# Layer 1's feed-forward with four gate and up pairs as seven products, and weight sums formed in layer 0: a one-core Trainium2 trunk

## The chip, the cores and the metric

The program runs on one core of one Trainium2 chip. The metric is device microseconds of the whole execution. The kernel before took 2606.74 us, the median of three runs (2606.5 to 2606.75). The profile is one further execution of it.

## The reference

A two-layer trunk over 256 tokens and 16 meta tokens in front of them, model width 2048, everything in float32:

```
h = concat(meta, x)                                  # 272 x 2048
h = h + ssd_mixer(rmsnorm(h))                        # layer 0: Mamba-2 SSD, inner width 4096
h = h + swiglu(rmsnorm(h), w_gate_up[0], w_down[0])
k, v = rmsnorm(h) @ w_kv                             # shared keys and values
h = h + stick_breaking_attention(rmsnorm(h), w_q, k, v, w_o)   # layer 1
h = h + swiglu(rmsnorm(h), w_gate_up[1], w_down[1])
out = rmsnorm(h)[16:]

swiglu(u, wgu, wd) = (silu((u @ wgu)[:, :5632]) * (u @ wgu)[:, 5632:]) @ wd
```

Layer 1's feed-forward, on 256 tokens, is where most of the change lies.

## The kernel before, in words

**Number format.** A float32 product is three TensorE products: each operand is split into a rounded part `hi` (type fp32r) and a remainder `lo`, and hi x lo, hi x hi and lo x hi are added up in PSUM. ScalarE makes a weight's `hi` (L128), VectorE its `lo` (L129). Tokens are split once per stage and stay in SBUF (`u`, `hid`).

**Weights.** Each weight block of 128 x 1024 (512 KB) comes by one DMA on SyncE's queue (SP) into one of five `raw` buffers (`load`, L111), is split into one of five `hi` and one of four `lo` buffers (`halves`), and serves 24 matmuls (`mac`, L142 to L144: eight pieces of 128 x 128, three each). A projection (`project`, L152) to 128 outputs has two blocks and 48 matmuls, each with the weight piece stationary and all tokens moving (272 columns in layer 0, 256 in layer 1's feed-forward). `project_block` does several projections side by side.

**Layer 0's feed-forward** (`ffn0`, L599) runs 44 gate and 44 up projections and the down projections in two parts of the hidden rows (`PARTS`). Each projection's split, products and collection follow one another in program order; SP, ACT, DVE and PE run ahead of each other as far as the buffers go. After the first block of a projection a caller may have something done (`then`).

**Layer 1's feed-forward** (L817 to the end) has two kinds of work interleaved:

- gate and up projections by `project` for hidden block m = 0 to 43, loop at L1034. Two neighbouring blocks make one hidden pair j = m // 2; `keep` (L874) forms the four token-and-row blocks of the pair, their sums (`sm`), and their `hi` and `lo` in the buffer `sa`.
- the down projection for a pair j of hidden rows and a group g of 512 output columns as a "quad": a product of two 2 x 2 block matrices in seven block products in place of eight (the scheme of Strassen and Winograd). Here the tokens (`sa`) are stationary and the weights, 256 columns, are moving. `quad` (L911) loads the weight's four blocks (`raw`), forms four differences of them on VectorE (`tt`, L918 to L920), splits blocks and differences (`split`, `less`, L892 to L900), and issues 7 x 3 = 21 matmuls (L904) into four PSUM banks `x0` to `x3`. A run of pairs (`RUNS`: 0 to 4, 5 to 10, 11 to 16, 17 to 21) stays in the banks; at its end `gather` (L955) combines the banks and adds to the residual `res`.

Which quad comes when is set by a small planner: `tick` is called twice per projection and `step` issues the next quad if its rows were kept at least `LAG` ticks ago and the running `debt` (an account with the entries of `WORK`) is below `ROOM`. The first ticks transpose the residual (`turn`, L842), since from then on tokens stand on partitions.

**The last run** (L1056 to the end, pairs 17 to 21) is written out by hand: for column group 0 quads, for groups 1 to 3 eight plain products (`plain`, `products`), with the final norm of the finished groups between them; `part` (L1115) does group 3 piece by piece, and `collect` (L968) adds each finished bank to the residual.

**Short matmuls.** `short` (L837) issues two matmuls of 128 columns at the first quad of each run's group 0 and behind each block of transposes in `turn`; `beat` (L147) issues three at chosen places of the projections.

**Element-wise lines named below**: L958 to L962 and L965 are the combination and the residual add in `gather`, L971 is `collect`, L990 the multiplication by the final norm's weight, L1073 the last scaling.

## Time and profile before

| | before |
|---|---|
| median of three runs | 2606.74 us |
| profiled execution | 2606.56 us |
| its span (first to last instruction) | 2604.8 us |
| mean granted TensorE clock | 0.999 |
| bytes moved | 482.5 MB, 185 GB/s on average |

The stages by the trace: state-space mixer to about 730 us, layer 0's feed-forward to about 1501 us, keys, values, attention and output projection to 1896 us, layer 1's feed-forward from there to the end, of which the last run from 2544 us.

How to read it: PE is TensorE's matmul, PEld its weight load, DVE is VectorE, ACT is ScalarE, POOL is GpSimd and SP is SyncE, whose queue (SPq) issues the DMAs. A matmul's row shows the time from its issue to its end; since matmuls overlap, what one costs is the step to the next one's start. A row of the groups of instructions has the line, engine, operation, tiles, the count, the busy time, the mean of one in ns, and the idle time of that engine ahead of them with what ended it.

### The profile page before, as it was taken

To read this page: it belongs to the slowest core of one execution; us is meant where nothing else is said; L and a number is where in the kernel's file an instruction comes from. 1 tells how busy PE (TensorE), PEld (TensorE's weight loads), DVE (VectorE), ACT (ScalarE), POOL (GpSimd) and SP (SyncE) were. 2 spreads that over 40 slices of the span, in tenths; PEclk is the share of its full clock that TensorE was granted. 3 is DMA by queue.
4 is the path that set the end of the run, shared out by engine and by line. 5 is a ranking of instruction groups with operands and counts; after the bars stand their busy time and mean duration, and the time that the engine had idled before them with its cause. 6 is when DMAs were issued, how large, how long until landed. Compare 5 with 4: busy or idle time off the path is not lost.

```text
span 2604.8 us, 52246 instructions
## 1 busy us (share of the span) xinstructions
PE 2595.8 (100%) x21767; PEld 2589.3 (99%) x21767; DVE 1838.8 (71%) x2777; ACT 1373.7 (53%) x1948; POOL 6.2 (0%) x26
## 2 busy tenths in 40 slices
PE   9999999999999999999999999999999999999998
PEld 9999999999999999999999999999999999999998
DVE  8888777768855554445555576666666988989998
ACT  6766657556544443334444454444554555555554
POOL 0000000000000000000000000000000000000000
PEclk9999999999999999999999999999999999999999
DMA  7666656565555555555555555555656656566665
GB/s 256 201 186 187 185 174 188 175 186 182 170 178 179 178 178 179 178 179 178 178 179 166 185 182 159 169 169 157 192 178 195 201 190 211 194 202 202 209 203 170
DMA packets 159597, 482.47 MB, mean 185 GB/s; under 512 B 21824, under 2 KB 43264, under 8 KB 159360
## 3 DMA queue, kind: packets, MB, share of 16 engines
q1 hardware_dynamic: 159072, 478.86, 58.3%
q8 instruction: 170, 2.79, 0.4%
q14 instruction: 67, 0.55, 0.1%
q10 hardware_dynamic: 288, 0.28, 0.0%
HBM read 476.91 MB, written 2.17 MB: 184 GB/s over the span
## 4 chain that ended last, share of the span: by engine, by line
PE 99%; ACT 0%; DVE 0%; DMA 0%; issue 0%; SPq 0%; DVEq 0%
PE pp L144 29%; PE pp L143 29%; PE pp L142 29%; PE x L904 7%; PE pp L904 1%; PE py L536 1%; PE py L542 0%; PE pt L449 0%; PE pb L725 0%; PE pt L319 0%; PE psc L694 0%; PE pe L143 0%; PE pe L142 0%; PE pe L144 0%; PE pc L491 0%; DMA raw<-w_first 0%
## 5 line engine op out<-in xcount | busy, mean ns | idle before, releaser
L128 ACT CAST hi<-raw 128x1024 fp32r<-128x1024 f32 (+1 forms) x802 | 832.6, 1041 | 899.9 <-PE pp L143 733.9
L129 DVE TENSOR_TENSOR lo<-raw,hi 128x1024 fp32r<-128x1024 f32 (+1 forms) x802 | 964.8, 1206 | 274.2 <-issue 121.5
L142 PE MATMUL pp<-u,hi 128*128 128x272 f32 (+1 forms) x4064 | 1147.8, 282 | 0.0
L143 PE MATMUL pp<-u,hi 128*128 128x272 f32 (+1 forms) x4064 | 1145.9, 282 | 0.0
L144 PE MATMUL pp<-u,lo 128*128 128x272 f32 (+1 forms) x4064 | 1145.4, 282 | 0.1
L143 PEld LDWEIGHTS pp<-u,hi 128*128 128x128 f32 x4064 | 763.0, 188 | 0.5 <-issue 0.4
L142 PEld LDWEIGHTS pp<-u,hi 128*128 128x128 f32 x4064 | 763.0, 188 | 0.4
L144 PEld LDWEIGHTS pp<-u,lo 128*128 128x128 f32 x4064 | 762.6, 188 | 0.5 <-DVE lo L129 0.3
L142 PE MATMUL pp<-hid,hi 128*128 128x272 f32 x704 | 201.7, 287 | 0.0
L144 PE MATMUL pp<-hid,lo 128*128 128x272 f32 x704 | 201.7, 287 | 0.0
L143 PE MATMUL pp<-hid,hi 128*128 128x272 f32 x704 | 201.7, 286 | 0.0
L904 PE MATMUL x<-hi,sa 128*128 128x256 f32 x1062 | 184.3, 276 | 0.0
L904 PEld LDWEIGHTS x<-hi,sa 128*128 128x128 f32 x1062 | 159.9, 188 | 0.0
L142 PE MATMUL pp<-ukv,hi 128*128 128x272 f32 x512 | 147.4, 288 | 0.0
L142 PE MATMUL pp<-y,hi 128*128 128x272 f32 x512 | 147.3, 288 | 0.0
L144 PE MATMUL pp<-y,lo 128*128 128x272 f32 x512 | 146.7, 287 | 0.0
L143 PE MATMUL pp<-y,hi 128*128 128x272 f32 x512 | 146.7, 286 | 0.0
L144 PE MATMUL pp<-ukv,lo 128*128 128x272 f32 x512 | 146.1, 285 | 0.0
L143 PE MATMUL pp<-ukv,hi 128*128 128x272 f32 x512 | 146.1, 285 | 0.0
L896 ACT CAST hi<-tt 128x1024 fp32r<-128x1024 f32 x73 | 76.8, 1052 | 123.4 <-PE pp L143 63.1
L144 PEld LDWEIGHTS pp<-hid,lo 128*128 128x128 f32 x704 | 132.6, 188 | 0.0
L142 PEld LDWEIGHTS pp<-hid,hi 128*128 128x128 f32 x704 | 132.6, 188 | 0.0
(302 smaller groups left out, 3612.6 us busy)
## 6 DMA issues: line engine op xcount, KB each, us to landing
raw<-w_gu SPq DMA_DIRECT2D x352, 512.0 KB, 3.6
raw<-w_in SPq DMA_DIRECT2D x152, 512.0 KB, 3.6
raw<-w_dn SPq DMA_DIRECT2D x88, 512.0 KB, 3.9
raw<-w_down SPq DMA_DIRECT2D x80, 512.0 KB, 3.4
raw<-w_out SPq DMA_DIRECT2D x64, 512.0 KB, 3.8
raw<-w_kv SPq DMA_DIRECT2D x64, 512.0 KB, 3.5
raw<-w_q SPq DMA_DIRECT2D x32, 512.0 KB, 3.5
raw<-w_o SPq DMA_DIRECT2D x32, 512.0 KB, 3.6
```

What stands on the lines that cost most here:

```text
L128: S.copy(hi[:, :n, :m], raw[:, :n, :m])
L129: V.tensor_tensor(out=lo[:, :n, :m], in0=raw[:, :n, :m], in1=hi[:, :n, :m].bitcast(F32), op=ALU.subtract)
L142: PE.matmul(ps[:, :n], wh, xl, start=first, stop=False)
L143: PE.matmul(ps[:, :n], wh, xh, start=False, stop=False)
L144: PE.matmul(ps[:, :n], wl, xh, start=False, stop=last)
L536: pin(PE.matmul(py[i * HD:(i + 1) * HD, c0:c1], xd[b][:, 2 * j + i, :], gm[b][:, 2 * j + i, :], start=True, stop=True))
L896: S.copy(hi[:, :n], src[:, :n])
L904: PE.matmul(ps, st[x][:, b], w[y][:, c], start=f, stop=l, skip_group_check=True)
```

## The change

**In layer 0's feed-forward**, 85 "jobs" are worked off. A job loads one block of layer 1's weights into a buffer `sr`, forms the same four differences of it as a quad does (`differences`, result `st`), and stores the 512 KB to DRAM (`sums`). `ahead` is called after the first weight block of each projection, and by `PACE` = 0.8 four calls in five take a job. 32 jobs are for the gate and up weights in a new layout (`w_sg`), 53 for blocks of `w_dn`.

**In layer 1**, the hidden pairs 3, 7, 11 and 15 (`SEVEN`) no longer get their gate and up values by `project`. `run_u` does such a pair as eight units of seven products, through the same function as a quad (`seven`), with the tokens of `u` and four sums of them (`us`, made by `form`) stationary and `w_sg` moving. `gated` combines the banks and applies silu and the product; `turned` transposes the result by four matmuls against `ident`, and `keep` goes on as before. Where a unit's differences were stored, `seven` loads three blocks of the weight (384 KB) and the stored differences (512 KB) instead of forming them.

**Plan and tail.** `RUNS` has six runs in place of four (the last with three pairs in place of five); `tick` may issue a second unit, by new entries in `WORK`; there are two `tt` buffers in place of three. Of the last run, all three rows of group 3 are now held and issued by `part`.

```diff
-RUNS = [(0, 5), (5, 11), (11, 17), (17, 22)]
-SLOTS = [42, 42]
+RUNS = [(0, 4), (4, 8), (8, 12), (12, 16), (16, 19), (19, 22)]
+SLOTS = [28, 28]
+SEVEN = [3, 7, 11, 15]
+SUMMED = [(g, j) for j in range(19) for g in range(3 if 4 <= j < 16 else 4) if g in (0, 2) or 4 <= j < 16 and g < 2] + [(0, j) for j in range(19, 22)]
-TT = 3
+TT = 2
+PACE = 0.8
-BEGIN = 5
-LAG = 3
+BEGIN = 8
+LAG = 2
...
+        sums = {}
+        jobs = [(a["w_sg"][i, q], (j, q, "u")) for i, j in enumerate(SEVEN) for q in range(KD // 2)]
+        jobs += [(a["w_dn"][g, j], (g, j)) for g, j in SUMMED]
+
+        def differences(raw, t):
+            V.tensor_tensor(out=t[:, 0:2], in0=raw[:, 3:4].to_broadcast([P, 2, BC]), in1=raw[:, 0:2], op=ALU.subtract)
+            V.tensor_tensor(out=t[:, 2], in0=raw[:, 1], in1=t[:, 0], op=ALU.subtract)
+            V.tensor_tensor(out=t[:, 3], in0=raw[:, 2], in1=t[:, 2], op=ALU.subtract)
...
+                def store():
+                    key, t = stored.pop(0)
+                    sums[key] = dp.tile([P, 4, BC], F32, name=nm("sum"))
+                    nc.sync.dma_start(sums[key], t)
+
+                def ahead():
+                    share[0] += PACE
+                    if share[0] < 1 or not jobs:
+                        return
+                    share[0] -= 1
+                    if stored:
+                        store()
+                    src, key = jobs.pop(0)
+                    raw = ft.tile([P, 4, BC], F32, tag="sr", name=nm("sr"))
+                    nc.sync.dma_start(raw, src.rearrange("(p b c) -> p b c", p=P, c=BC))
+                    t = ft.tile([P, 4, BC], F32, tag="st", name=nm("st"))
+                    differences(raw, t)
+                    stored.append((key, t))
...
-                        times(gt, tile_pair(gu, m, u, pre), rB)
+                        times(gt, tile_pair(gu, m, u, pre, ahead), rB)
...
-            def quad(xs, g, j, first, last):
...
+            def seven(xs, src, key, st, shift, first, last, wake):
+                ready = sums.get(key)
+                raw = fetch(src, 4 if ready is None else 3)
+                t = quarter() if ready is None else fetch(ready)
+                w1 = split(raw, 3, True, shift)
+                if ready is None:
+                    differences(raw, t)
                 less(raw, w1, 3)
-                w2 = split(t, 4)
+                w2 = split(t, 4, shift=shift)
                 less(t, w2, 4)
-                if first and g == 0:
+                if wake:
                     short(xs[3][:, 1, :P])
...
+            def gated(xs):
+                e, f = combine(xs)
+                y = [sp.tile([P, T], F32, tag="sq", name=nm("y"))[:, :BC] for _ in range(2)]
+                for t in range(2):
+                    S.activation(f[:, t], e[:, 2 * t], AF.Silu, scale=rt[:, t:t + 1])
+                for t in range(2):
+                    V.tensor_tensor(out=y[t], in0=e[:, 2 * t + 1], in1=f[:, t], op=ALU.mult)
+                return y
+
+            def turned(j, y):
+                ps = pp.tile([P, 512], F32, tag="pp", name=nm("pt")).rearrange("p (b t) -> p b t", t=P)
+                for i, (f, t) in enumerate(((0, 1), (0, 0), (1, 0), (1, 1))):
+                    pin(PE.transpose(ps[:, i], y[t][:, f * P:(f + 1) * P], ident))
+                up = quarter().rearrange("p b (s t) -> p (b s) t", t=P)[:, :4]
+                S.copy(up, ps)
+                keep(j, up)
...
+            def run_u(j):
+                x = [bank(i) for i in range(4)]
+                n = KD // 2
+                for q in range(n):
+                    seven(x, source(a["w_sg"][SEVEN.index(j), q]), (j, q, "u"), lambda b: given(q, b), SHIFT_U,
+                          q == 0, q == n - 1, q == 0)
+                    if q == n - 1:
+                        y = gated(x)
+                        debt[0] += WORK["gated"] - WORK["gather"] + 2.3
+                        later.append((ticks[0] + WAIT, lambda: turned(j, y)))
+                    yield j, True
...
-            for m in range(KF):
+            for m in [2 * j + i for j in range(KF // 2) if j not in SEVEN for i in range(2)]:
...
-            for f in (f1, f1, f1, f0, f1, f0, f1, f0):
+            for f in (f1, f1, f0, f1, f0):
...
-            for j in range(j0, j1 - 4):
-                plain(c3, 3, j, j == j0, False)
-            held = [(j, whole(3, j)) for j in range(j1 - 4, j1)]
+            held = [(j, whole(3, j)) for j in range(j0, j1)]
```

On SP in layer 0's gate and up stage, between two weight loads there now often stands a job's load or the store of the job before it.

On PE in layer 1's feed-forward, where a run begins with a short pair (L839). Before (`pp<-u` is a gate or up projection, `x<-lq,sa` a quad):

```order
L144 MATMUL pp_22996<-u_21431,lo_23057 128x256
L839 MATMUL x_3098_23089<-u_21431 128x128 x2
L904 MATMUL x_3098_23089<-lq_23093,sa_22824 128x256
L904 MATMUL x_3098_23089<-hi_23094,sa_22824 128x256 x2
L904 MATMUL x_23086<-lq_23093,sa_22824 128x256
```

Now, at the first unit of a gate and up pair (stationary `u` and `us`):

```order
L151 MATMUL pp_24322<-u_22111,lo_24356 128x256
L882 MATMUL x_3449_24388<-u_22111 128x128 x2
L960 MATMUL x_3449_24388<-lq_24393,u_22111 128x256
L960 MATMUL x_3449_24388<-hi_24394,u_22111 128x256 x2
L960 MATMUL x_24385<-lq_24393,u_22111 128x256
L960 MATMUL x_24385<-hi_24394,u_22111 128x256 x2
L960 MATMUL x_24387<-lq_24393,us 128x256
L960 MATMUL x_24387<-hi_24394,us 128x256 x2
```

And now, behind the pair's last unit, at the transposes of its result (`pt<-ident,y`), inside a projection:

```order
L150 MATMUL pp_24457<-u_22111,hi_24460 128x256
L151 MATMUL pp_24457<-u_22111,lo_24461 128x256
L1046 MATMUL pt_24488<-ident,y_24316 128x128
L1046 MATMUL pt_24488<-ident,y_24315 128x128 x2
L1046 MATMUL pt_24488<-ident,y_24316 128x128
L149 MATMUL pp_24457<-u_22111,hi_24506 128x256
L150 MATMUL pp_24457<-u_22111,hi_24506 128x256
```

A gate and up pair is entered with a short pair like a run; its transposes stand inside a projection, and the projection goes on behind them without one.

On DVE at the end, from the combination of the last gather (`tt<-x`) to the collection of the last group's first bank. Before:

```order
L960 TENSOR_TENSOR tt_31393<-x_31050,tt_31393 128x512
L900 TENSOR_TENSOR lo_31475<-raw_31473,hi_31476 128x1024
L961 TENSOR_TENSOR tt_31392<-x_31050,tt_31393 128x256
L962 TENSOR_TENSOR tt_31392<-x_31051,tt_31393 128x512
L900 TENSOR_TENSOR lo_31505<-raw_31503,hi_31506 128x1024
L965 SCALAR_TENSOR_TENSOR h<-tt_31392,rt,h 128x512 x2
L900 TENSOR_TENSOR lo_31511<-raw_31509,hi_31512 128x1024
L990 TENSOR_TENSOR h<-h,gf_31432 128x512 x2
L971 SCALAR_TENSOR_TENSOR h<-pp_31220,rt,h 128x512
L900 TENSOR_TENSOR lo_31517<-raw_31515,hi_31518 128x1024
L971 SCALAR_TENSOR_TENSOR h<-pp_31221,rt,h 128x512
```

Now:

```order
L1029 TENSOR_TENSOR tt_32430<-x_32223,tt_32430 128x512
L956 TENSOR_TENSOR lo_32488<-raw_32486,hi_32489 128x1024
L1030 TENSOR_TENSOR tt_32429<-x_32223,tt_32430 128x256
L1031 TENSOR_TENSOR tt_32429<-x_32224,tt_32430 128x512
L956 TENSOR_TENSOR lo_32494<-raw_32492,hi_32495 128x1024
L1055 SCALAR_TENSOR_TENSOR h<-tt_32429,rt,h 128x512 x2
L1061 SCALAR_TENSOR_TENSOR h<-pp_32324,rt,h 128x512
L1080 TENSOR_TENSOR h<-h,gf_32469 128x512 x2
L1080 TENSOR_TENSOR h<-h,gf_32516 128x512
L1061 SCALAR_TENSOR_TENSOR h<-pp_32325,rt,h 128x512
L1199 TENSOR_REDUCE sd<-ss 128x1
```

Two splits (`lo`) stand behind the start of the gather's combination where there were five (the fifth, of the same kind, some rows further on), and the collections follow one another with fewer of them between.

More of the change, by code (lines that the diff above doesn't have):

```diff
@@ L46 @@
 SHIFT = 48
+SHIFT_U = 32
 RAW = 5
-TT = 3
+TT = 2
 START = 1
-BEGIN = 5
-LAG = 3
+PACE = 0.8
+BEGIN = 8
+LAG = 2
 ROOM = 0.3
-WORK = {"half": 1.27, "unit": 1.1, "gather": 3.7, "keep": 2.0}
+ROOM_S = 1.2
+MORE = 0.6
+WORK = {"half": 1.42, "unit": 0.9, "summed": -0.3, "gather": 3.5, "keep": 2.0, "gated": 0.7}
+WAIT = 3
 LQ = 2
@@ L621, in ffn0 @@
                     for m in range(FILLERS, KD):
-                        done(m, project(srcs[m], hid))
+                        done(m, project(srcs[m], hid, then=ahead))
+                while stored:
+                    store()
+                assert not jobs
         ukv = [None]
@@ L872, in where, with four @@
                 return part, w, (j - RUNS[part][0]) * w
+            def four(up, sm, hi, lo):
+                V.tensor_tensor(out=sm[:, 0], in0=up[:, 0], in1=up[:, 3], op=ALU.add)
+                V.tensor_tensor(out=sm[:, 2], in0=up[:, 0], in1=up[:, 1], op=ALU.subtract)
+                V.tensor_tensor(out=sm[:, 1], in0=sm[:, 0], in1=up[:, 1], op=ALU.subtract)
+                V.tensor_tensor(out=sm[:, 3], in0=up[:, 2], in1=sm[:, 1], op=ALU.subtract)
+                S.copy(hi, sm)
             def keep(j, up):
                 part, w, at = where(j)
+                while any(k < 0 and p == part - 2 for k, p, _ in work):
+                    step(True)
                 hi, lo = slot(part)
@@ new lines, in kept, with given, fetch @@
+            def kept(j, b):
+                part, w, at = where(j)
+                return [x[:, at + b] for x in slot(part)]
+            def given(q, b):
+                if b > 2:
+                    return [us[:, x, 4 * q + b - 3] for x in range(2)]
+                k, t = ((0, 0), (1, 0), (1, 1))[b]
+                return [u[x][:, 2 * q + k, t * P:(t + 1) * P] for x in range(2)]
+            def fetch(src, n=4):
+                raw = wp.tile([P, LC, P], F32, tag="raw", name=nm("raw"), bufs=RAW)
+                raw = raw.rearrange("p (b k) c -> p b (k c)", b=4)
+                nc.sync.dma_start(raw[:, :n], src[:, :n])
+                return raw
@@ L929, in quad @@
                                        (xs[1][:, 1], 5, w2, 1, False)):
-                    three(ps, st, at + b, w, c, first and f, last)
+                    three(ps, st(b), w, c, first and f, last)
+            def quad(xs, g, j, first, last):
+                w = where(j)[1]
+                seven(xs, source(dn[g, j]), (g, j), lambda b: kept(j, b + w - 7), SHIFT, first, last, first and g == 0)
             def whole(g, j):
-                raw = fetch(g, j)
+                raw = fetch(source(dn[g, j]))
                 w1 = split(raw, 4)
@@ L943, in products @@
                 ps, apart = (cs[t][c], True) if isinstance(cs[t], tuple) else (cs[t][:, c], c == 0)
-                three(ps, st, at + b1, w1, c1, first and apart, False)
-                three(ps, st, at + b2, w1, c2, False, last)
+                three(ps, kept(j, b1), w1, c1, first and apart, False)
+                three(ps, kept(j, b2), w1, c2, False, last)
             def plain(cs, g, j, first, last):
@@ L1006, in step @@
                     return False
-                p, g = work[0]
+                k, p, g = work[0]
                 if going[0] is None:
-                    going[0], going[1] = run(p, g), RUNS[p][0]
-                j, last = going[1], going[1] == RUNS[p][1] - 1
-                if not free and (j >= len(made) or made[j] + LAG > ticks[0] or debt[0] > ROOM
-                                 or last and ticks[0] % 8 not in (3, 4, 5, 6)):
+                    going[0], going[1] = (run(p, g), RUNS[p][0]) if k < 0 else (run_u(k), 0)
+                j, last = going[1], going[1] == (RUNS[p][1] if k < 0 else KD // 2) - 1
+                if k < 0 and free and j not in made:
+                    flush(True)
+                room = ROOM_S if k >= 0 or (g, j) in sums else ROOM
+                if not free and (k < 0 and made.get(j, 1000) + LAG > ticks[0] or debt[0] > room):
                     return False
-                next(going[0])
+                _, ready = next(going[0])
                 going[1] += 1
-                debt[0] += WORK["unit"]
+                debt[0] = max(0.0, debt[0] + WORK["summed" if ready else "unit"])
                 if last:
@@ L1021, in step, with flush @@
                 return True
+            def flush(free=False):
+                while later and (free or later[0][0] <= ticks[0]):
+                    later.pop(0)[1]()
             def tick():
```

97 lines of the change are left out of this document (55 added, 42 removed).

## The prediction

> **What bounds the kernel now.** I read the page's busy table and its chain that ended last first, then the busy time by stretch (start and end of the stretch; busy time and instruction count of PE, PEld, DVE, ACT, POOL; granted clock; DMA share; GB/s).
>
> ```profile
> PE 2595.8 (100%) x21767; PEld 2589.3 (99%) x21767; DVE 1838.8 (71%) x2777; ACT 1373.7 (53%) x1948; POOL 6.2 (0%) x26
> ...
> PE 99%; ACT 0%; DVE 0%; DMA 0%; issue 0%; SPq 0%; DVEq 0%
> ```
>
> ```profile
> 10.00:20.00 10.00, 9.88 (x79) 9.57 (x78) 9.90 (x20) 10.00 (x22) 0.00 (x0) 1.00 1.04 392
> 725.00:1000.00 275.00, 275.00 (x2230) 274.92 (x2229) 150.35 (x187) 117.17 (x142) 0.00 (x0) 1.00 0.57 179
> 1940.50:2540.00 599.50, 599.50 (x5292) 599.50 (x5291) 525.66 (x776) 331.06 (x390) 0.00 (x0) 1.00 0.62 200
> 2596.90:2604.80 7.90, 0.17 (x2) 0.00 (x0) 2.98 (x9) 0.81 (x3) 0.00 (x0) 0.69 0.52 194
> ```
>
> In layer 1's feed-forward (third row) PE starts 5292 matmuls in 599.5 us, 113.3 ns each, and is never idle; DVE works 526 of the 600 us, and the chain is PE alone. So what counts is the number of matmuls times that step, plus whatever disturbs the step. Layer 0's gate and up stage (second row) has DVE 45% idle and moves 179 GB/s.
>
> The step has two values. The timeline of PE (start, duration, line, operation):
>
> ```profile
> 1908.06 0.28 PE L143 MATMUL pp<-u,hi 128*128 128x256 f32 x1
> ...
> 1919.25 0.34 PE L150 MATMUL beat<-u,hi 128*128 128x128 f32 x2
> ```
>
> These 95 matmuls of 256 columns (two times 48, less the first) took 11.19 us, 117.8 ns each, with the clock at 1.00. They follow a plain fp32 matmul; the three short matmuls (`beat`) end the state. Slow against fast is 4.5 ns a matmul.
>
> **The change part by part.** *Products.* A pair of gate and up columns cost 4 projections x 16 x 3 = 192 matmuls and now costs 8 x 7 x 3 = 168: four pairs save 96. The last run of down rows shrinks from five to three, so two rows turn from eight products to seven in three column groups: 2 x 3 x 3 = 18 more. 114 x 113.3 ns = 12.9 us less.
>
> *Transposes and short pairs.* Four groups of four transposes (`turned`) and six more pairs of shorts come in. Their prices:
>
> ```profile
> 1929.08 0.60 PE L848 MATMUL x<-ident,h 128*128 128x128 f32 x4
> 1929.51 0.38 PE L854 MATMUL rp<-ident,rB 128*128 128x128 f32 x2
> 1929.65 0.37 PE L142 MATMUL pp<-u,hi 128*128 128x256 f32 x1
> 1929.86 0.28 PE L143 MATMUL pp<-u,hi 128*128 128x256 f32 x1
> ```
>
> ```profile
> 2176.05 0.33 PE L839 MATMUL x<-u 128*128 128x128 f32 x2
> 2176.22 0.33 PE L904 MATMUL x<-lq,sa 128*128 128x256 f32 x1
> 2176.39 0.40 PE L904 MATMUL x<-hi,sa 128*128 128x256 f32 x2
> 2176.63 0.28 PE L904 MATMUL x<-lq,sa 128*128 128x256 f32 x1
> ```
>
> Transposes step by 0.109 us, the last by about 0.03, and the first product behind them by 0.21 instead of 0.11: a group costs 3 x 0.109 + 0.03 + 0.10 = 0.46, four cost 1.8 us. The Trainium skill ("TensorE: Matmul & The Clock Gate", Part 4) puts one 128x128 transpose at about 275 ns in a kernel's context. By that figure sixteen would cost 4.4 us and the forecast would stand 2.6 us later; the rows here do not show such a step. A short pair costs 0.17, the product behind it 0.06 and two more 0.01 extra: 0.24 us, six cost 1.4 us.
>
> *What follows the transposes.* In the kernel before, a short pair followed each block of transposes in this stage. Behind the new ones there is none until the next run's pair: by the changed order 294, 870, 750 and 726 matmuls of 256 columns. If transposes leave PE in the slow step, that is 2640 x 4.5 ns = 11.9 us; if not, nothing. Two rows of precedent, where 256-wide products follow fp32 work with no shorts:
>
> ```profile
> 1806.53 0.49 PE L725 MATMUL pb<-ident,sc 128*128 128x128 f32 x3
> 1806.77 0.36 PE L142 MATMUL pp<-ob,hi 128*128 128x256 f32 x1
> 1806.97 0.28 PE L143 MATMUL pp<-ob,hi 128*128 128x256 f32 x1
> ...
> 1807.44 0.28 PE L144 MATMUL pp<-ob,lo 128*128 128x256 f32 x1
> ```
>
> ```profile
> 1817.17 0.39 PE L746 MATMUL po<-bd,vsT 128*128 128x128 f32 x2
> 1817.31 0.37 PE L142 MATMUL pp<-ob,hi 128*128 128x256 f32 x1
> 1817.52 0.28 PE L143 MATMUL pp<-ob,hi 128*128 128x256 f32 x1
> ...
> 1817.86 0.28 PE L143 MATMUL pp<-ob,hi 128*128 128x256 f32 x1
> ```
>
> The first went slow (four steps in 0.47 us), the second fast (three in 0.34). The rows at 1929.65 look like the second: 0.21, then 0.11. So the nearer precedent is fast. I take none or one of the three long stretches (3.3 to 3.9 us each) as slow, half of one, 1.7 us, and keep 0 and 11.9 for the range.
>
> *Differences moved to layer 0.* The rows of the groups of instructions (count | busy, mean ns | idle before):
>
> ```profile
> L129 DVE TENSOR_TENSOR lo<-raw,hi 128x1024 fp32r<-128x1024 f32 (+1 forms) x802 | 964.8, 1206 | 274.2 <-issue 121.5 <-PE pp L144 116.9 <-ACT hi L128 20.1
> L900 DVE TENSOR_TENSOR lo<-tt,hi 128x1024 fp32r<-128x1024 f32 x73 | 89.2, 1222 | 10.1 <-ACT hi L896 9.8
> L900 DVE TENSOR_TENSOR lq<-raw,hi 128x768 fp32r<-128x768 f32 x73 | 69.7, 955 | 0.1
> L918 DVE TENSOR_TENSOR tt<-raw 128x512 f32<-128x512 f32 x73 | 50.2, 691 | 15.0 <-DMA raw<-w_dn 14.9
> L920 DVE TENSOR_TENSOR tt<-raw,tt 128x256 f32<-128x256 f32 x73 | 31.0, 424 | 1.2
> L965 DVE SCALAR_TENSOR_TENSOR h<-tt,rt,h 128x512 f32<-128x512 f32 x26 | 18.3, 749 | 0.0
> L960 DVE TENSOR_TENSOR tt<-x,tt 128x512 f32<-128x512 f32 x13 | 8.9, 682 | 0.0
> ```
>
> One set of differences is 0.69 + 2 x 0.42 = 1.54 us of DVE; 85 sets put 131 us into layer 0, at nine sets to twenty weight blocks (the order). A block is 24 matmuls, and 2230 started in 275 us, so twenty blocks are 59 us, in which DVE has 27 us idle and gets 14. Priced at nothing; the cover is the idle 45%. Behind a difference that waits for its load, DVE holds back the next `lo`, and PE waits for that only after four blocks, about 11 us. Bytes: twenty blocks then move 38 transfers of 0.52 MB, 19.9 MB in 59 us, 336 GB/s; 392 were moved at 10 to 20 us. Of stores nothing this size is shown; were they twice as dear as loads, nine more transfers make 416 GB/s, 6% over that rate, and layer 0 would lose up to 35 us over 560. Loads and stores of like width should cost alike, so I take nothing. An issue on SP's queue:
>
> ```profile
> 2043.05 0.33 SPq L908 DMA_DIRECT2D raw<-w_dn  x1
> ```
>
> In layer 0, 170 more (85 loads, 85 stores) are 56 us of SP; with a weight block's own, a block comes to 1.9 x 0.33 = 0.63 of its 2.95 us. A store waits on SP for the last of its three subtractions and holds the weight loads behind it; it stands one `ahead` later than the subtractions, so it should find them done, and PE's lead of some four blocks covers the rest. If not, it is a gap in PE of a us or so at each of 85 stores' places at worst; I take nothing.
>
> *DVE in layer 1.* Gone: 47 sets, 72 us. New: 12 more combinations at 2 x 0.68 + 3 x 0.42 = 2.6 (31 us), 16 more L965 at 0.75 (12), 38 more `lq` at 0.955 (36), the eight `form` and the gate products about 18, less some 7 of `gt` and `up`: 18 us more, against 74 us idle in the third row. DVE goes from 88 to about 91% busy there. Nothing on the path; bound 0 to 3 us of short PE waits, since the new units come in pairs.
>
> *The end.* DVE's timeline in the last run:
>
> ```profile
> 2575.20 0.42 DVE L958 TENSOR_TENSOR tt<-x,tt 128x256 f32<-128x256 f32 x1
> 2575.53 0.42 DVE L959 TENSOR_TENSOR tt<-x,tt 128x256 f32<-128x256 f32 x1
> 2575.86 0.68 DVE L960 TENSOR_TENSOR tt<-x,tt 128x512 f32<-128x512 f32 x1
> 2576.46 1.22 DVE L900 TENSOR_TENSOR lo<-raw,hi 128x1024 fp32r<-128x1024 f32 x1
> 2577.59 0.42 DVE L961 TENSOR_TENSOR tt<-x,tt 128x256 f32<-128x256 f32 x1
> ...
> 2591.67 0.75 DVE L971 SCALAR_TENSOR_TENSOR h<-pp,rt,h 128x512 f32<-128x512 f32 x1 [3.17 <-PE pp L904]
> ...
> 2597.11 0.48 DVE L971 SCALAR_TENSOR_TENSOR h<-x,rt,h 128x256 f32<-128x256 f32 x1
> ```
>
> From the last gather (2575.20, when PE ends group 0) to the collection of the last bank (2591.67) DVE works 16.5 - 3.2 = 13.3 us; a `lo` takes 1.13 of it. The changed order has two `lo` there instead of five: 9.9 us. PE used to have 192 matmuls from that point, 21.8 us, and now has 120, 13.6 us; the collection waits for the 84th, 9.5 us. So DVE's 3.2 us of slack is gone, and from there its own chain (2591.67 to the span's end at 2604.8, 13.1 us) sets the end: 9.9 + 13.1 = 23.0, or 23.5 with a wait for ACT's squares, against 13.6 + 7.9 = 21.5 by PE (7.9 is the last stretch of the table, behind PE's last long matmul). That gives back 1.5 to 2.0; I take 1.8.
>
> *Sum.* 12.9 less 1.8, 1.4, 1.8 and 0.1 (24 more slow steps beside the second `turn`) is 7.8. The profiled execution took 2606.56 (span 2604.8, the rest lies around it; the median of the runs is 2606.74): 2598.8, and with 1.7 for the step 2600.5.
>
> **The rivals.** *Slow step throughout (slower).* The transposes leave PE slow each time, and so do the changes to and from the new runs, whose operands stand at other addresses: 11.9 us, and 4.5 ns x about 1220 matmuls of those runs, 5.5 us. 2598.8 + 11.9 to 17.4 = 2611 to 2616. It decides from 13 us on, some 2900 slow matmuls. For it: 1806.97 and 1908.06; against it: 1817.52, and that the pairs of shorts have always reset the step. With two of three long stretches slow the time is 2598.8 + 7 = 2606, no change.
>
> *Too few raw buffers (slower).* Transfers of the stretch 2000 to 2540:
>
> ```profile
> DMA to landing us min/median/max: 3.3/4.0/6.0
> ```
>
> A pair of summed units and a half projection (66 matmuls, 7.5 us) uses five weight buffers, and there are five. Each is held 4.0 + 1.05 (ACT) + 1.22 (DVE) = 6.3 us, so 1.2 us is left. Above a landing of 5.2 us PE loses the excess in each of some 37 pairs, once its lead is used up. At 6.0 this is 0.8 a pair, mostly hidden; at 7 it is 1.8 a pair, and with a third of it showing 22 us: 2620. The demand in such a pair is 2.36 MB in 7.5 us, 315 GB/s, below the 392 shown, which speaks against it. The Trainium skill ("DMA: Bandwidth & Descriptors", Latency and other measured facts) gives HBM access 0.2 us on average and 2 us at high load. By that rule landing could come to 5.8, just over the edge.
>
> *DVE or nothing gained.* The sums come back too late or the gathers crowd DVE, so the saved matmuls turn into PE waits: 2603 to 2607.
>
> **How the numbers follow.** What can be told from no change is 0.2%, 5.2 us, so faster is below 2601.5. Forecast case with zero to one slow stretch: 0.55, 2597 to 2603, most of it below that line. Two slow stretches, or waits of like size: 0.22, about 2606. Slow throughout: 0.13. Buffers or stores: 0.06. Better than the sum (no loss at the end): 0.04, 2596.5. Faster 0.58, same 0.25, slower 0.17. The range 2596.5 to 2609 leaves out the slow ends.
>
> **What would show it.** Right: the third stretch's step stays at 113.3 ns behind the `pt` rows; DMA share near 0.9 with PE unbroken in layer 0; DVE without its 3.2 us of idle before the last bank's collection, and some 10 us in place of 7.9 between PE's last long matmul and the end. Wrong: runs of 117.8 ns behind `pt`; PE waiting for `hi` or `lo` in the paired units, with landings above 5 us; PE gaps before 1300 us.

## The result

The changed kernel takes 2630.05 us (median of four runs, 2627.35 to 2633.88) against 2606.74: 1.0091 times the time before, 95% interval 1.0073 to 1.0108. It is slower by 23 us, where 6 us less were forecast. The profiled execution is the one of 2633.88 us, with a span of 2632.2, 27.4 us longer than before's; it is the longest of the four, so the account below explains some 4 us more than the medians differ by.

The page of the changed kernel, busy times and the chain that ended last:

```profile
PE 2605.5 (99%) x21681; PEld 2593.4 (99%) x21681; DVE 1961.4 (75%) x3037; ACT 1408.6 (54%) x2026; POOL 6.2 (0%) x26
...
PE 79%; DMA 10%; DVE 8%; issue 2%; ACT 1%; SPq 0%; DVEq 0%; ACTq 0%
```

PE has 86 instructions less, as planned, but the chain is no longer PE alone: DMA and DVE hold 18% of it. Where the time went, by the first product of each stage in the two traces:

| stage (us) | before | changed | difference |
|---|---|---|---|
| layer 0's feed-forward | 782.0 | 800.6 | +18.6 |
| keys, values, attention, output projection | 395.1 | 395.0 | -0.1 |
| layer 1's feed-forward, to PE's last product | 700.2 | 708.2 | +8.0 |
| from there to the end | 8.1 | 8.9 | +0.8 |

**Layer 0.** What DVE waited for there (us in total, times, longest), and below it DVE's timeline around the longest stall of PE:

```profile
DVE st L613 <- DMA sr<-w_dn: 111.3, 33, 5.4
DVE st L613 <- DMA sr<-w_sg: 47.1, 15, 6.1
```

```profile
951.03 2.35 DVE L136 TENSOR_TENSOR lo<-raw,hi 128x1024 fp32r<-128x1024 f32 x2
958.78 0.69 DVE L613 TENSOR_TENSOR st<-sr 128x512 f32<-128x512 f32 x1 [5.40 <-DMA sr<-w_dn]
959.50 0.43 DVE L614 TENSOR_TENSOR st<-sr,st 128x256 f32<-128x256 f32 x1
960.11 0.69 DVE L613 TENSOR_TENSOR st<-sr 128x512 f32<-128x512 f32 x1 [0.18 <-DMA sr<-w_dn]
...
961.41 1.22 DVE L136 TENSOR_TENSOR lo<-raw,hi 128x1024 fp32r<-128x1024 f32 x1
```

SP's queue and PE at the same place:

```profile
951.20 0.90 SPq L636 DMA_DIRECT2D sr<-w_dn  x2
```

```profile
960.50 0.28 PE L150 MATMUL pp<-u,hi 128*128 128x272 f32 x1
962.68 0.39 PE L151 MATMUL pp<-u,lo 128*128 128x272 f32 x1 [1.90 <-DVE lo L136]
```

DVE stands 5.4 us at a subtraction whose load went out at 951.2 and landed 7 us later. The weight split behind it comes at 961.41, PE has used up its lead by 960.5 and waits 1.9 us. A median load of this kind takes 6.9 us (`sr<-w_dn`), where weights took 3.5 in this stage before; PE has eighteen such stalls, 18.6 us with the steps around them.

**Layer 1.** Two things cost time. First, waits. What ACT waited for in this stage, and ACT's and DVE's timelines ahead of the longest wait of PE:

```profile
ACT hi L952 <- DVE tt L615: 35.5, 13, 7.4
ACT gt L1161 <- DVE gt L194: 34.2, 17, 6.0
```

```profile
2461.95 0.84 ACT L952 CAST hi<-raw 128x768 fp32r<-128x768 f32 x1 [0.24 <-DMA raw<-w_dn]
2468.45 0.42 ACT L1161 ACTIVATE gt<-gt 128x256 f32<-128x256 f32 x1 [5.67 <-DVE gt L194]
2469.80 1.04 ACT L952 CAST hi<-tt 128x1024 fp32r<-128x1024 f32 x1 [0.92 <-DVE tt L615]
2470.75 1.04 ACT L135 CAST hi<-raw 128x1024 fp32r<-128x1024 f32 x1
```

```profile
2462.89 0.42 DVE L1027 TENSOR_TENSOR tt<-x,tt 128x256 f32<-128x256 f32 x1
...
2466.07 1.41 DVE L1055 SCALAR_TENSOR_TENSOR h<-tt,rt,h 128x512 f32<-128x512 f32 x2
2467.40 0.68 DVE L613 TENSOR_TENSOR tt<-raw 128x512 f32<-128x512 f32 x1
2468.00 0.42 DVE L194 TENSOR_TENSOR gt<-pp,rB 128x256 f32<-128x256 f32 x1
...
2470.06 0.42 DVE L615 TENSOR_TENSOR tt<-raw,tt 128x256 f32<-128x256 f32 x1
```

```profile
2468.73 0.39 PE L960 MATMUL x<-hi,sa 128*128 128x256 f32 x2
2471.84 0.39 PE L149 MATMUL pp<-u,hi 128*128 128x256 f32 x1 [2.72 <-ACT hi L135]
```

The combination of a finished group (L1027 to L1055) holds DVE from 2462.9 to 2467.4 and both `tt` buffers. Only then come the next units' differences, and between them a gate product (`gt`, L194) for which ACT stands 5.67 us. Then come ACT's cast of the differences and, behind that in ACT's queue, the cast for which PE waits. ACT's waits for `gt` are as long in sum as those for differences. After this wait PE's steps are 213 ns from 2472.7 to 2476.1, at a granted clock of 0.50. The Trainium skill ("TensorE: Matmul & The Clock Gate", Part 1) has a clock of 1.2 GHz after an idle window of about 3.4 us, by which 256 columns take an estimated 213.3 ns; the trace agrees on the step, though the wait was only 2.7 us.

Second, the slow step. Two stretches of the changed kernel (columns as in the prediction's table of stretches; the counts hold one or two products that overlap the edges):

```profile
2073.70:2152.90 79.20, 79.20 (x675) 79.20 (x674) 73.02 (x104) 44.55 (x54) 0.00 (x0) 1.00 0.68 227
2284.97:2342.20 57.23, 57.23 (x507) 57.23 (x506) 52.45 (x80) 33.32 (x43) 0.00 (x0) 1.00 0.76 267
```

Both without a gap: 117.7 ns a product in the first (673), 113.3 in the second (505). The trace of layer 1 has 2016 products of 256 columns with the slow step, against 135 before.

**The account.** For each kernel below I counted in layer 1's trace the *waits* (time above 113.3 ns where a product starts over 128 ns after the one before, products right behind short matmuls and transposes left out; the 213 ns steps count) and the *slow* products (steps of 116.6 to 120.5 ns). Stage less waits less 4.5 ns a slow product is 700.2 - 0.3 - 0.6 = 699.3 us before and 708.2 - 9.4 - 9.1 = 689.7 after. The kernels e1 to e6, e9 and e10 below, which differ in plans and buffers, give 689.6 to 689.8 by the same sum. So the saved products, with transposes and shorts paid, are worth 9.6 us, and waits and slow steps, with those of before taken off, take 17.6 away.

| kernel | median (us) | layer 0 | layer 1 to PE's last | waits | slow |
|---|---|---|---|---|---|
| before | 2606.74 | 782.0 | 700.2 | 0.3 | 135 |
| changed | 2630.05 | 800.6 | 708.2 | 9.4 | 2016 |
| e1 pinned | 2612.43 | 782.0 | 705.4 | 6.4 | 2078 |
| e2 later, pinned | 2612.68 | 782.0 | 708.4 | 10.1 | 1901 |
| e3 one tile | 2628.43 | 800.4 | 701.8 | 5.7 | 1425 |
| e4 pinned, one tile | 2608.07 | 782.0 | 700.4 | 4.3 | 1418 |
| e5 spaced, two tiles | 2609.19 | 782.0 | 701.7 | 4.5 | 1669 |
| e6 spaced, one tile | 2611.10 | 782.0 | 706.0 | 3.8 | 2816 |
| e8 no sums | 2687.73 | 782.0 | 777.0 | 74.3 | 2132 |
| e9 101 jobs, spaced | 2610.75 | 782.0 | 705.6 | 1.7 | 3177 |
| e10 101 jobs | 2613.29 | 782.0 | 701.9 | 4.6 | 1676 |
| e11 with triples | 2610.47 | 782.0 | 701.0 | 2.5 | 875 |

The medians are of all runs, the other columns of one profile each, and that execution is not always a middle one: e6's took 2613.84 us, e9's 2614.64 (the longest of its eleven), e10's 2609.47 and e11's 2608.34. So the columns of those rows don't add up to their medians. The changed kernel, e1 and e2 have the same layer 1, and their profiles show 6.4 to 10.1 us of waits; a difference smaller than that between two kernels is no evidence. The kernel before was run beside each of them and stayed at 2606.6 to 2606.8.

### The profile page after: what moved, and what is told of

It reads as the page before. It is cut to its first block, busy times and chain, and to the rows that moved or that the text cites. A ratio compares the mean times of both kernels' runs of the same rounds, so it can differ in the third digit from the quotient of the medians.

```text
span 2632.2 us, 53089 instructions
## 1 busy us (share of the span) xinstructions
PE 2605.5 (99%) x21681; PEld 2593.4 (99%) x21681; DVE 1961.4 (75%) x3037; ACT 1408.6 (54%) x2026; POOL 6.2 (0%) x26
## 4 chain that ended last, share of the span: by engine, by line
PE 79%; DMA 10%; DVE 8%; issue 2%; ACT 1%; SPq 0%; DVEq 0%; ACTq 0%
PE pp L151 22%; PE pp L149 22%; PE pp L150 22%; PE x L960 9%; DMA sr<-w_dn 6%; DVE lo L136 3%; DMA sr<-w_sg 2%; DVE st L613 1%; ACT hi L135 1%; DMA raw<-w_gu 1%; DVE st L614 1%; PE py L545 1%; PE pp L960 1%; DVE lo L956 0%; PE py L551 0%
## 5 line engine op out<-in xcount | busy, mean ns | idle before, releaser
L135 ACT CAST hi<-raw 128x1024 fp32r<-128x1024 f32 (+1 forms) x770 | 792.1, 1038 | 694.4 <-PE pp L150 467.7
L151 PE MATMUL pp<-u,lo 128*128 128x272 f32 (+1 forms) x3808 | 1080.2, 284 | 10.1 <-DVE lo L136 9.8
L149 PE MATMUL pp<-u,hi 128*128 128x272 f32 (+1 forms) x3808 | 1081.2, 284 | 3.7 <-ACT hi L135 3.7
L150 PE MATMUL pp<-u,hi 128*128 128x272 f32 (+1 forms) x3808 | 1078.6, 283 | 0.0
L136 DVE TENSOR_TENSOR lo<-raw,hi 128x1024 fp32r<-128x1024 f32 (+1 forms) x770 | 922.1, 1204 | 171.2 <-PE pp L151 70.4
L151 PEld LDWEIGHTS pp<-u,lo 128*128 128x128 f32 x3808 | 716.8, 188 | 13.7 <-DVE lo L136 13.5
L149 PEld LDWEIGHTS pp<-u,hi 128*128 128x128 f32 x3808 | 716.2, 188 | 4.5 <-ACT hi L135 4.3
L150 PEld LDWEIGHTS pp<-u,hi 128*128 128x128 f32 x3808 | 716.8, 188 | 0.5 <-issue 0.4
L952 ACT CAST hi<-raw 128x768 fp32r<-128x768 f32 (+1 forms) x205 | 190.3, 934 | 96.2 <-PE pp L150 47.7
L960 PE MATMUL x<-hi,sa 128*128 128x256 f32 x1130 | 197.9, 278 | 0.0
L613 DVE TENSOR_TENSOR st<-sr 128x512 f32<-128x512 f32 x85 | 58.7, 690 | 162.7 <-DMA sr<-w_dn 111.3
L960 PEld LDWEIGHTS x<-hi,sa 128*128 128x128 f32 x1130 | 171.8, 189 | 0.0
```

Of the source, the lines that this page charges most:

```text
L135: S.copy(hi[:, :n, :m], raw[:, :n, :m])
L136: V.tensor_tensor(out=lo[:, :n, :m], in0=raw[:, :n, :m], in1=hi[:, :n, :m].bitcast(F32), op=ALU.subtract)
L149: PE.matmul(ps[:, :n], wh, xl, start=first, stop=False)
L150: PE.matmul(ps[:, :n], wh, xh, start=False, stop=False)
L151: PE.matmul(ps[:, :n], wl, xh, start=False, stop=last)
L613: V.tensor_tensor(out=t[:, 0:2], in0=raw[:, 3:4].to_broadcast([P, 2, BC]), in1=raw[:, 0:2], op=ALU.subtract)
```

## The experiments

**e1 and e2: layer 0's subtractions held at their place.** The program's scheduler orders each engine's instructions by its own estimate of when their data is there. It had put the jobs' subtractions early: the last one runs at 1265 us, while the last job is written in the stage that begins at 1402. `pin` (keep in program order) holds an instruction behind all that was written before it on its engine.

```diff
-            V.tensor_tensor(out=t[:, 0:2], in0=raw[:, 3:4]..., in1=raw[:, 0:2], op=ALU.subtract)
+            i = V.tensor_tensor(out=t[:, 0:2], in0=raw[:, 3:4]..., in1=raw[:, 0:2], op=ALU.subtract)
+            if hold:
+                pin(i)
```

In e2, `ahead` also forms the differences of the job loaded one call earlier:

```diff
+                    if loaded:
+                        formed()
                     src, key = jobs.pop(0)
...
-                    differences(raw, t)
-                    stored.append((key, t))
+                    loaded.append((key, raw))
```

> The first subtraction of each layer 0 job is held at its place in the written order on DVE (the scheduler had put it ahead of weight splits, as soon as its own estimate had the load landed). Same loads, same stores, same bytes. Theory Q (queue): PE's 20 stalls in layer 0 come from DVE standing at a subtraction whose load has not landed, with the weight splits behind it; then layer 0's feed-forward goes from 800.6 to 782-786 us, DVE's idle time ahead of the subtraction from 163 us to under 40, and the run to 2612-2616. Rival R (rate): the loads and stores together are too much for the DMA engines at some 320 GB/s and the weights land too late; then layer 0 stays at 797-803, PE waits for hi and lo behind raw loads, and the run stays at 2627-2634.

> As the run before it, and each job's subtractions also come one job later than its load (about 7 us more). Theory Q: 782-784 us in layer 0, no stall left, the run at 2611-2614; if it is clearly better than the pinned kernel, the load's landing of about 7 us was still too long for the first. Rival R: no change, 2627-2634.

e1 took 2612.43 us (1.0019 times before, 1.0009 to 1.0028), e2 2612.68. Layer 0 is back to 782.0 us in both. The same stretch in the changed kernel and in e1:

```profile
770.00:1000.00 230.00, 223.44 (x1777) 221.34 (x1777) 159.54 (x249) 85.67 (x110) 0.00 (x0) 0.99 0.89 318
```

```profile
770.00:1000.00 230.00, 230.00 (x1867) 230.00 (x1866) 169.70 (x249) 96.67 (x117) 0.00 (x0) 1.00 0.92 320
```

At the same 320 GB/s, DMA share of 0.9 and 249 DVE instructions, PE loses 6.6 us in the first and nothing in the second. Over a longer time the edit also spreads the jobs: 58 in place of 73 run from 760 to 1260 us, and the last at 1482. That this is not what helped is shown by e9 below, which has 101 jobs and moves more in this stretch, with PE unbroken:

```profile
770.00:1000.00 230.00, 230.00 (x1867) 230.00 (x1866) 173.67 (x262) 93.42 (x115) 0.00 (x0) 1.00 0.94 336
```
 What DVE waits for in e1's layer 0 no longer has a row for the subtraction; its group has no idle time at all, where the changed kernel had 162.7 us:

```profile
L613 DVE TENSOR_TENSOR st<-sr 128x512 f32<-128x512 f32 x85 | 58.3, 686 | 0.0
```

The queue's order was the whole of layer 0's loss; the rate (rival R) was not. A median load still takes 6.2 us in e1. Coming another job later (e2) adds nothing.

**e3 and e4: the combination in one tile.** The same operations, in place, so that one `tt` buffer stays free (e4 has e1's edit too).

```diff
-                e, f = quarter(), quarter()
-                S.copy(f[:, 3], xs[3][:, 0])
-                V.tensor_tensor(out=f[:, 0], in0=xs[0][:, 1], in1=f[:, 3], op=ALU.add)
-                V.tensor_tensor(out=e[:, 0], in0=xs[0][:, 0], in1=f[:, 3], op=ALU.add)
+                e = quarter()
+                S.copy(e[:, 3], xs[3][:, 0])
+                V.tensor_tensor(out=e[:, 0], in0=xs[0][:, 0], in1=e[:, 3], op=ALU.add)
+                V.tensor_tensor(out=e[:, 3], in0=xs[0][:, 1], in1=e[:, 3], op=ALU.add)
...
```

> The combination at a run's end works in one tt tile in place of two (same operations), so that one of the two tt buffers stays free for the next unit's differences. Layer 0 as in the changed kernel. Theory T (buffers): PE's waits in layer 1's feed-forward (10.8 us beyond the step in 56 gaps, most of them within 10 us behind a combination, ACT standing 5 to 7 us at the cast of a difference) go to under 4 us, and with them most of the 1210 slow matmuls that follow waits: the stage from 717 to 700-704 us, slow matmuls from 2016 to under 1100, the run at 2613-2618. Rival P (plan): DVE has too much to do in these places whatever the buffers; then waits stay over 7 us and the run over 2624. Rival A (transposes and addresses): the slow step does not follow the waits; then over 1700 slow matmuls stay and the run is at 2620-2624.

> Both edits of the first and the third run. Theories Q and T together: 2630 less 17 less 14, 2596-2602, faster than the kernel before. Q alone 2612-2616, T alone 2613-2618, neither 2627-2634. If the two do not add up, they share a cause.

e3 took 2628.43 us, e4 2608.07 (1.0005 times before, 0.9996 to 1.0014: no difference that can be told). Neither reached its number. One tile is worth 4 us where both kernels ran on one chip (2612.43 to 2608.07), a third of what theory T gave it. Waits of 5.7 and 4.3 us stay, and 1420 slow products. ACT's longest waits went from 7.4 to 4.7 us for a difference and from 6.0 to 3.2 for `gt`, but the total for differences did not fall (e3):

```profile
ACT hi L952 <- DVE tt L615: 44.3, 19, 4.7
ACT gt L1161 <- DVE gt L194: 27.4, 19, 3.2
```

So the buffer was a part; the group's combination and the next group's differences still crowd each other on DVE.

**e5 and e6: more products between the groups.** Only the planner's account is changed, on e1 and on e4.

```diff
-WORK = {"half": 1.42, "unit": 0.9, "summed": -0.3, "gather": 3.5, "keep": 2.0, "gated": 0.7}
+WORK = {"half": 1.5, "unit": 0.9, "summed": -0.3, "gather": 4.5, "keep": 0.8, "gated": 0.7}
```

> On the pinned kernel, the planner's account alone is changed (half 1.42 to 1.5, gather 3.5 to 4.5, keep 2.0 to 0.8): by the order at least 72 gate and up products (8.2 us) now stand behind the end of each group where it was often 48 (5.4 us); the combination still works in two tt tiles. Theory P (plan): PE's waits in layer 1 come from the next group starting before the combination is through; then the waits (gaps not behind short matmuls or transposes) fall under 2 us, slow matmuls under 1200, the run to 2601-2604. Theory T (buffers): with both tt buffers held by the combination the next differences, their cast and their split still come one after another, 5.5 + 1.5 + 1.0 + 1.2 = 9.2 us, over the 8.2; then some 5 us of waits stay and the run is at 2607-2611.

> As the run before it, with the combination in one tt tile. Theories P and T together: waits under 1 us, some 850 slow matmuls left (those around the gate and up pairs that run as seven products), layer 1's feed-forward 694 us to PE's last product and 9 behind, the run at 2601-2603, faster than the kernel before by 0.2%. Rival D (DVE has too much to do in layer 1 as such): the waits only move, 3 us or more, and the run stays at 2605-2608.

e5 took 2609.19 us with 4.5 us of waits, as its theory T has it: more products between the groups did not free the buffers. e6 took 2611.10 us with 3.8 us of waits, against theories P and T together; the waits are of rival D's size, the time lies above that rival's range. In e6 the three longest waits, 3.0 us of the 3.8, stand at one kind of place, the ninth product of a unit that forms its own differences. Its slow products are 2816, twice e4's.

**e8: no sums.** All differences are formed in layer 1; layer 0 has no jobs.

```diff
-                ready = sums.get(key)
+                ready = None
...
-        jobs = [(a["w_sg"][i, q], (j, q, "u")) for i, j in enumerate(SEVEN) for q in range(KD // 2)]
-        jobs += [(a["w_dn"][g, j], (g, j)) for g, j in SUMMED]
+        jobs = []
```

> As the spaced kernel with one tile, but no jobs in layer 0: all differences are formed in layer 1 (131 us of DVE more there), the rest of the plan the same. If the sums are what makes room for the seven-product pairs, DVE becomes the bound of layer 1: 585 + 131 us of work in 600 us, 20 to 60 us of PE waits and slow steps, 2625-2665. Rival N (not needed: DVE's idle time was enough): within 5 us of the spaced kernel.

2687.73 us (1.0312 times before), 77 us over e6, more than expected. ACT's longest sum of waits and PE's own:

```profile
ACT hi L953 <- DVE tt L616: 181.8, 59, 5.6
```

```profile
PE x L961 <- DVE lo L957: 26.8, 18, 5.1
PE pp L149 <- ACT hi L135: 16.7, 15, 2.6
```

So the stored sums do what they are for: with none of the 85 the seven-product pairs don't pay.

**e9 and e10: 16 more sums.**

```diff
-SUMMED = [(g, j) for j in range(19) for g in range(3 if 4 <= j < 16 else 4) if g in (0, 2) or 4 <= j < 16 and g < 2] + [(0, j) for j in range(19, 22)]
-PACE = 0.8
+SUMMED = [(g, j) for j in range(19) for g in range(3 if 12 <= j < 16 else 4) if j < 16 or g in (0, 2)] + [(0, j) for j in range(19, 22)]
+PACE = 0.95
```

> On the spaced kernel with one tile: 101 jobs in layer 0 in place of 85 (PACE 0.95 for 0.8), so that 16 more of the down-projection units find their differences stored; 25 us less of DVE in layer 1. In the runs so far what waits of PE are left stand at the ninth product of a unit that forms its differences itself. Theory D (DVE has too much to do around those units): the waits go from 3.8 us to under 1.5, the slow matmuls behind them with them (under 1100), layer 1 to PE's last product 692-696 us, the run at 2600-2603. Rival L (loads): summed units bring 0.92 MB for 42 + 24 products and the weights now land late; waits for hi behind raw loads, 4 us or more, the run over 2606. Rival R once more (rate in layer 0): 341 GB/s there is too much, stalls come back, layer 0's feed-forward over 786 us.

> The same 101 jobs on the pinned one-tile kernel with the changed kernel's own plan (48 products behind a group's end where the spaced plan has 72). Theory P: the combination is not through in 5.4 us and waits of 0.4 to 1 us stay at the first unit of groups, some 3 to 5 us in all, the run at 2603-2607; if it is as fast as the spaced one, the spacing is worth nothing and the stored differences are what counts.

e9 has 1.7 us of waits left, close to theory D's 1.5, and the profile names no wait of PE in layer 1 any more. But the median is 2610.75 us, and slow products went to 3177, 14.3 us, in the profiled execution. e10, with the tighter plan, keeps 4.6 us of waits as theory P has it, but takes 2613.29, above that theory's range. The runs of the two overlap (2606.62 to 2614.64 and 2607.45 to 2615.80), so which plan is better isn't settled. In layer 0 even 101 jobs cost nothing (782.0 us at 312 GB/s over the stage).

In e9 the slow stretches begin in three ways: at a change between gate and up products and a unit of a seven-product pair, at a wait (of 0.1 us here, of 1 us in e6), and behind a short pair that stands directly behind transposes. This last, in e9:

```profile
2233.70 0.60 PE L1048 MATMUL pt<-ident,y 128*128 128x128 f32 x4
2234.06 0.42 PE L884 MATMUL x<-u 128*128 128x128 f32 x2
2234.31 0.33 PE L962 MATMUL x<-lq,sa 128*128 128x256 f32 x1
2234.48 0.40 PE L962 MATMUL x<-hi,sa 128*128 128x256 f32 x2
2234.72 0.28 PE L962 MATMUL x<-lq,sa 128*128 128x256 f32 x1
2234.84 0.40 PE L962 MATMUL x<-hi,sa 128*128 128x256 f32 x2
2235.07 0.28 PE L962 MATMUL x<-lq,sa 128*128 128x256 f32 x1
2235.19 0.40 PE L962 MATMUL x<-hi,sa 128*128 128x256 f32 x2
2235.43 0.28 PE L962 MATMUL x<-lo,sa 128*128 128x256 f32 x1
```

From 2234.72 to 2235.43 six products take 0.71 us, 118 ns each: slow, in spite of the short pair. Once slow, it stays until the next break.

**e11: triples of short matmuls.** On e9, triples at the start of projections (fourteen in the trace; the expectation counted thirteen), one more matmul each than a short pair, written into the projection's own bank:

```diff
+                if k0 == 0 and beats == 2:
+                    for w, s in ((hi, 0), (hi, 1), (lo, 0)):
+                        PE.matmul(o[:, 3 * P:], w[:, 0, :], x[s][:, 0, :P], start=True, stop=True, skip_group_check=True)
...
```

> On the kernel with 101 jobs and the spaced plan: thirteen triples of short matmuls (as `beat`, into a free part of the projection's own bank) between gate and up projections, at the first projection after a run's groups 0 and 2 begin and after each block of transposes. That kernel has 3177 slow products of 256 columns in layer 1 and only 1.7 us of waits. Theory B (a triple between equal products always ends the slow step): every long stretch behind a triple is fast, slow products fall under 2000, and the stage to PE's last product goes from 705.6 to 703-705 (13 x 0.34 us more, 1200 or more x 4.5 ns less). Rival C (chance: any break draws the state anew): some triples are followed by slow stretches, over 2400 slow products stay, and the stage takes 707-712.

875 slow products in place of 3177, stage 701.0 us: better than expected. Every one of the fourteen triples is followed by a fast stretch, five of them out of a slow one, as theory B has it. But most of the fall is not the triples' work. In e9 three stretches of 643, 715 and 751 slow products, 2109 in all, begin at waits of 0.1 us (at 2121, 2374 and 2481 us). In e11 the same units have waits of the same size at the same products, the nearest triple ahead stands some 10 us or more earlier, and fast products follow. From the first of these places on, to where e11 has its next triple, e9 and then e11:

```profile
2121.55:2149.80 28.25, 28.25 (x241) 28.25 (x241) 24.63 (x31) 16.82 (x20) 0.00 (x0) 1.00 0.77 263
```

```profile
2123.30:2149.80 26.50, 26.50 (x237) 26.50 (x236) 23.48 (x29) 16.46 (x19) 0.00 (x0) 1.00 0.76 270
```

That is 117.7 ns a product against 113.3. So a wait of this size is followed by either step, as rival C has it for any break, and e11's profile had the fast one three times: for the most part luck. The triples cost some 4.9 us (701.0 - 2.5 - 3.9 = 694.6, against 689.7), and the median, 2610.47 (2608.16 to 2612.35), is near e9's 2610.75: a gain of the triples in the time isn't shown.

**e7, e12 and e13: the addresses.** On e6, the moving weights of the seven-product pairs are shifted in their buffers. Between a moving operand and the next stationary one lie 64 bytes modulo 256 in all other long stretches, by the places of the buffers in the built program; the traces hold no addresses.

```diff
-SHIFT_U = 32
+SHIFT_U = 48
```

(16 in e12, 0 in e13)

> As the run before it, with the moving weights of the gate and up units 64 bytes further on in their buffers (SHIFT_U 48 for 32). Theory A (addresses): the step's state is set by where stationary and moving operands stand to each other modulo 256 bytes (64 in all long stretches, 0 on entering and 128 on leaving a unit); now it is 0 inside a unit and 64 on leaving it: the 672 products of the units take another step than 113.3 ns, and the projections behind them keep the state they had. Rival S (sequence): it is the change of the kind of work as such; then steps and flips are as in the run before.

> On the spaced kernel with one tile: the moving weights of the gate and up units 64 bytes further back (SHIFT_U 16), so that stationary and moving operand stand 128 apart modulo 256 inside the units, where 0 gave only slow steps and 64 gave mostly fast ones. Theory A (addresses): the step inside the units is again one value of its own, the same in all four pairs. Rival S (sequence): mixed as at 64.

> The same with SHIFT_U 0: 192 apart inside the units. Theory A: one value again in all four pairs; if it is 113.3 from the first product on, 64 is not the best place. Rival S: mixed as at 64.

Two units of 21 products stand one behind the other, 42 in all. The same places, up to three for each kernel, one fence each for e6 (64 apart), e7 (0), e12 (128) and e13 (192):

```profile
1957.04:1961.82 4.78, 4.78 (x44) 4.78 (x43) 3.57 (x4) 3.95 (x5) 0.00 (x0) 1.00 0.81 278
1964.65:1969.43 4.78, 4.78 (x44) 4.78 (x43) 3.19 (x3) 3.75 (x4) 0.00 (x0) 1.00 0.86 290
```

```profile
1957.29:1962.32 5.03, 5.03 (x44) 5.03 (x43) 3.71 (x5) 3.97 (x5) 0.00 (x0) 1.00 0.74 272
1965.15:1970.19 5.04, 5.04 (x45) 5.04 (x43) 3.33 (x4) 3.76 (x4) 0.00 (x0) 1.00 0.78 268
```

```profile
1957.12:1962.10 4.98, 4.98 (x44) 4.98 (x43) 3.68 (x5) 3.98 (x5) 0.00 (x0) 1.00 0.83 263
```

```profile
1956.81:1961.57 4.76, 4.76 (x44) 4.76 (x43) 3.56 (x4) 3.96 (x5) 0.00 (x0) 1.00 0.80 252
1964.40:1969.35 4.95, 4.95 (x44) 4.95 (x43) 3.15 (x3) 3.71 (x4) 0.00 (x0) 1.00 0.92 315
1972.08:1976.85 4.77, 4.77 (x45) 4.77 (x43) 3.88 (x4) 4.17 (x5) 0.00 (x0) 1.00 0.89 320
```

Divided by 42: at 64 113.8 ns here, and 117.8 in other places; at 0 always about 120; at 128 118.6, but 120 where two of the four pairs are entered; at 192 by turns 113.4 and 117.9, the first of each pair slow. So the addresses decide which steps there can be (theory A, for 0 and 128). At 64 and 192 there are two, and that the sequence decides between them (rival S) fits the turns but isn't shown by itself. By the step 64 is the best of the four. The single runs took 2610.88, 2614.82 and 2613.70 us, too near to e6's runs (2608.44 to 2614.26) to rank the four by time.

## Why the prediction was wrong

**Right.** The terms of PE's own work held: 12.9 less, 1.8 for transposes and 1.4 for shorts make 9.7, and the account above gives 699.3 - 689.7 = 9.6. The transposes' price, at the second of their four places:

```profile
2050.73 0.60 PE L1046 MATMUL pt<-ident,y 128*128 128x128 f32 x4
2051.09 0.37 PE L149 MATMUL pp<-u,hi 128*128 128x256 f32 x1
2051.29 0.28 PE L150 MATMUL pp<-u,hi 128*128 128x256 f32 x1
```

0.56 us from the first transpose to the second product, less one step of 0.11, is 0.45 us a group, as reckoned. The 275 ns that the Trainium skill ("TensorE: Matmul & The Clock Gate", Part 4) gives for a transpose is near what one takes from issue to end here: 0.60 us for the four, less three steps of 0.11, is 0.27. Since they overlap, it is not what one costs, and the price of 4.4 us for sixteen did not come. The transposes did not leave PE slow at any of the four places, which was the case taken. The end gave back 0.8 us, less than the 1.8: from PE's last long product to the end it takes 8.9 us, not some 10. DVE's slack before the last bank is gone, as forecast.

**Wrong: "Differences moved to layer 0 ... Priced at nothing; the cover is the idle 45%".** This is the step that failed, 18.6 of the 27.4 us. The cover was counted as idle time of DVE, but DVE works in order: what counts is how long its first instruction waits. I named that ("DVE holds back the next `lo`, and PE waits for that only after four blocks, about 11 us") and compared the lead with nothing: no landing of a job's load stands in the sum. It takes 6.9 us in the median, two jobs came back to back, and the scheduler had put the subtractions right behind the issue of their loads. The lead was shorter, too: at the longest stall the last `lo` was done at 953.4 us and PE had used it up by 960.6, 7.2 us later. PE gaps before 1300 us, one of the prediction's own signs of being wrong, are what came. The rate, which I did price, was no limit: the 336 GB/s worked out stand against 318 to 329 in the trace, and e1 (320) and e9 (336) move as much without a stall.

**Wrong: "I take none or one of the three long stretches ... half of one, 1.7 us".** Slow products cost 9.1 us less the 0.6 of before. The size is near the rival "slow step throughout" (11.9 to 17.4 us), which held 0.13; its mechanism was half right. Changes to and from the new runs do switch the step, not the transposes; the larger part, some 1200 of the 2016, lies in stretches that begin at a wait of PE (673 products behind the one at 2073). That "the pairs of shorts have always reset the step" is false: behind transposes, and ahead of a seven-product unit, they did not.

**Wrong: "Nothing on the path; bound 0 to 3 us of short PE waits".** 9.4 us. DVE's share was reckoned over the stage, and there it is right: 540 us of 620 (87%) in the changed kernel. The waits stand at group ends, where combination, differences and casts follow one another through two queues. That is what the third rival has ("the gathers crowd DVE"), and it was put at 2603 to 2607, without the slow products that the waits bring. "Too few raw buffers" was not it: the long waits are for differences, not for loads. In layer 1 the median landing went from 4.0 to 4.4 us. In layer 0 it went from 3.5 to 5.9 us for weights and was 6.9 for the jobs. By the rule of the Trainium skill ("DMA: Bandwidth & Descriptors", Latency and other measured facts: 0.2 us on average, 2 us at high load) an estimate for layer 0 is 3.5 + 1.8 = 5.3 us, and the trace has more.

**Open.** What in a wait or a change of work decides between the two steps at 64 bytes isn't settled: the same short pair behind the same transposes is followed by fast products in one place and slow ones in another, and the same wait by slow ones in e9 and fast ones in e11. Nor was a version found that beats the kernel before: e4 equals it (1.0005), e9 with neither waits nor slow steps would, by an estimate from its profile, take 16 us less than the 2614.64 of that execution, but no edit tried here gets rid of both.

## What to carry to other kernels

Idle time of an engine is no cover for work that waits for data: ask how long the first instruction in its queue stands, and what is behind it; and look where the scheduler puts that instruction, not where it is written. A kernel in which PE never pauses can hold a fast step for 600 us; a change that saves products but brings pauses can lose more by the step behind each pause than by the pause. Cost a new access pattern by the addresses of its operands too.

## What the runs showed of the hardware

- A step of 256 columns with fp32r operands takes 113.3 or 117.8 ns at the full clock. Which of them can occur depends on the distance, modulo 256 bytes, from a moving operand to the next stationary one: in the seven-product units 64 and 192 allow both, 0 gave about 120 ns, and 128 gave 118.6 or 120.
- The slow step lasts until something breaks the stream: 673 products in the changed kernel. A triple of 128-column matmuls between like projections ended it five times out of five, and none of e11's fourteen triples was followed by it at once. A wait of 0.1 us began it in e9 and did not in e11, at the same places.
- After a wait of 2.7 us the granted clock was 0.50 for 3.4 us, 213 ns a step of 256 columns (the changed kernel, 2472.7 to 2476.1 us).
- Loads and stores together moved 320 GB/s (e1) and 336 GB/s (e9) for 230 us with nothing lost on PE. In e1 a 512 KB load of a job then took 6.2 us in the median and one of weights 5.3, where a weight load took 3.5 at 179 GB/s before.
